# A stream of 774 unread matrix products behind the output of a two-layer transformer block

## The chip, the cores and the metric

The kernel runs on one core of one Trainium2 chip. The metric is device time in microseconds (us) of one execution. Before the change it is 1582.73 us, the median of 2 runs (1582.6 and 1582.87).

## The reference, cut to what matters

Two layers act on 512 tokens of width 1024 (`x`) and 256 context tokens (`ctx`). Layer 0 mixes tokens by a Fourier transform and a long convolution, layer 1 by latent attention; each is followed by a gated feed-forward part. Only `x` is returned.

```python
def _conv_ffn(h, w_up, conv_w, conv_b, w_down):
    gate, val = jnp.split(h @ w_up, 2, axis=-1)
    return (jax.nn.silu(_dwconv3(gate, conv_w, conv_b)) * val) @ w_down
...
        x = x + g1 * yx
        x = x + g2 * _conv_ffn(_modulate(_rms_norm(x, norm2[i]), sh2, sc2), *ffn)
...
    return x
```

The output depends on nothing that the change adds.

## The kernel before, in words

Activations lie with the 1024 channels on partitions, as eight row tiles of 128 channels each, and the tokens along the free axis. Layer 0 carries 512 tokens and 256 context tokens side by side, layer 1 from its attention on 512 tokens alone.

Nearly every product is done three times in a shortened float format (fp32r): a value is split into a high and a low part, and `mm3` (L214 to L218) issues high weight by high activation (L216), high weight by low activation (L217) and low weight by high activation (L218). Each is one weight load of 128x128 and one matmul of 512 or 256 columns. In the profile the names `wh` and `wl` are the two parts of a weight, `hh` and `hl` those of a normalised activation, `hhc` and `hlc` the same for the context, `ah` and `al` (`ahc`, `alc`) those of the feed-forward's inner activation, `Oh` and `Ol` those of the attention's output, `yh` and `yl` those of the mixer's; `mm` is a PSUM tile and `xr` a row tile of the residual.

The feed-forward part `ffn` is a loop over 22 inner tiles and two weight matrices. In layer 0 its products run in this order:

```python
                todo = [(k, q, a, n) for q in range(2) for a, n in segs for k in range(KD)]
```

`segs` is (512 columns, then 256 columns) there, so that for one weight tile 8 x 3 = 24 products of 512 columns (long ones) are followed by 24 of 256 columns (short ones), and so on, block after block.

The kernel's last work is the residual projection of layer 1 (`res_proj`, from L1167): for each of the eight row tiles products of 512 columns accumulate, then VectorE adds the result to `xr` at L1212. `build` issues one output DMA for each row tile from SyncE (L1847), then closes the pools in the reverse order of their opening. A pool is a stretch of SBUF or PSUM; closing it lets a later pool take the place, and the framework puts a semaphore wait wherever an instruction of a new tile must follow one on the old tile. On each engine instructions stand in the order in which the code issues them.

Of the kernel before, what the change touches and what calls it, by code (L numbers as in the profile page):

```python
# [9 lines left out]
F32 = mybir.dt.float32  # L10
F32R = mybir.dt.float32r
BF16 = mybir.dt.bfloat16
# [4 lines left out]
PSUM = bass.MemoryType.PSUM  # L17

P = 128
# [118 lines left out]
class Builder:  # L138
# [1703 lines left out]
    def build(self):  # L1842
        nc = self.nc
        self.setup()
        x = self.layer1(*self.layer0())
        for d in range(KD):
            nc.sync.dma_start(self.out[d], x[d][:, 0:T])  # L1847
        for n in ("xres", "h2p", "nt", "fit", "dx", "dr", "psA", "sm", "W", "P0"):
            self.close(n)

# [192 lines left out]
```

## Time and profile before

| | |
|---|---|
| median of 2 runs | 1582.73 us |
| profiled execution, its own time | 1584.1 us |
| its span, first to last instruction | 1582.3 us |
| TensorE busy | 1544.9 us, 98% of the span, 8360 matmuls |
| VectorE busy | 1028.8 us |
| ScalarE busy | 608.4 us |
| mean granted TensorE clock | 0.994 |

How to read it: "PE" is TensorE's matmul, "PEld" its weight load, DVE VectorE, ACT ScalarE, SP SyncE. A matmul's row has a start and a duration; successive matmuls overlap, since each duration contains a drain, so the pace of a stream is the distance from start to start, which I call the pitch. "PEclk" is the share of its full clock that TensorE was granted.

### The profile page before, as it was taken

The numbers are of one execution on the slowest core, as the hardware profiler recorded it, in microseconds if no ns is written. First come the engines' busy times: TensorE is split into PE (matmuls) and PEld (weight loads), VectorE is DVE, ScalarE is ACT, GpSimd is POOL, SyncE is SP. The second block draws the span as 40 slices with busy tenths as digits, with TensorE's granted clock in tenths as the row PEclk, the third lists the DMA queues.
The fourth block names the chain that finished last, engine by engine and source line by source line (L and its number), as shares of the span: only waits on it lengthen the run. The fifth ranks groups of instructions, "written<-read, shape, count | busy, mean of one in ns | idle before, by whom it ended". The sixth has DMA issues, their size and how long they took to land.

```text
span 1582.3 us, 21019 instructions
## 1 busy us (share of the span) xinstructions
PE 1544.9 (98%) x8360; PEld 1270.1 (80%) x8360; DVE 1028.8 (65%) x1740; ACT 608.4 (38%) x878; POOL 92.0 (6%) x109
## 2 busy tenths in 40 slices
PE   7999999999999999999999999999999999999999
PEld 4687888888888888888888887655459888888887
DVE  5788969878987356653364487898867544444343
ACT  4451224424332112322133247988843432233231
POOL 0013125000000000000000000111200000000000
PEclk9999999999999999999999999999999999999999
DMA  9336522543544234442353221000043232223222
GB/s 354 106 108 208 177 63 74 185 135 98 169 160 147 67 118 164 159 134 67 94 163 100 94 63 30 1 14 14 1 146 108 94 104 97 93 95 105 94 81 93
DMA packets 54542, 173.04 MB, mean 109 GB/s; under 512 B 6187, under 2 KB 9581, under 8 KB 53421
## 3 DMA queue, kind: packets, MB, share of 16 engines
q1 hardware_dynamic: 54445, 171.71, 32.8%
q8 instruction: 66, 1.08, 0.3%
q14 instruction: 31, 0.25, 0.1%
HBM read 165.91 MB, written 5.77 MB: 108 GB/s over the span
## 4 chain that ended last, share of the span: by engine, by line
PE 85%; DVE 10%; ACT 2%; DMA 2%; issue 1%; SPq 1%; POOL 0%; ACTq 0%; DVEq 0%
PE mm L216 23%; PE mm L218 23%; PE mm L217 23%; PE pv L1713 3%; PE s L1659 3%; DVE junk L301 2%; DVE wl L196 2%; PE pv L1724 1%; PE s L216 1%; PE k L216 1%; PE s L218 1%; PE s L217 1%; PE k L218 1%; PE k L217 1%; DVE hl L371 1%
## 5 line engine op out<-in xcount | busy, mean ns | idle before, releaser
L191 ACT ACTIVATE wh<-wr 128x1024 fp32r<-128x1024 f32 (+1 forms) x192 | 198.4, 1035 | 554.5 <-PE mm L217 508.4
L216 PE MATMUL mm<-hh,wh 128*128 128x512 f32 (+1 forms) x872 | 339.1, 390 | 2.5 <-ACT hh L367 0.9
L217 PE MATMUL mm<-hl,wh 128*128 128x512 f32 (+1 forms) x872 | 337.6, 387 | 2.3 <-DVE hl L371 2.3
L218 PE MATMUL mm<-hh,wl 128*128 128x512 f32 (+1 forms) x872 | 337.2, 387 | 1.6 <-DVE wl L196 1.6
L196 DVE TENSOR_TENSOR wl<-wr,wh 128x1024 fp32r<-128x1024 f32 (+2 forms) x192 | 230.5, 1203 | 140.8 <-ACT wh L191 136.6
L216 PEld LDWEIGHTS mm<-hh,wh 128*128 128x128 f32 x872 | 164.9, 189 | 35.5 <-issue 3.2
L218 PEld LDWEIGHTS mm<-hh,wl 128*128 128x128 f32 x872 | 165.0, 189 | 35.1 <-DVE wl L196 2.2
L217 PEld LDWEIGHTS mm<-hl,wh 128*128 128x128 f32 x872 | 165.1, 189 | 32.7 <-DVE hl L371 3.5
L301 DVE SCALAR_TENSOR_TENSOR junk<-wr,sb 128x1024 bf16<-128x1024 f32 x128 | 156.0, 1219 | 53.8 <-DMA wr<-wmodT 53.6
L1212 DVE SCALAR_TENSOR_TENSOR xr<-mm,mod,xr 128x512 f32<-128x512 f32 (+1 forms) x100 | 61.7, 630 | 170.1 <-PE mm L218 170.0
L217 PE MATMUL mm<-hlc,wh 128*128 128x256 f32 (+1 forms) x488 | 137.4, 282 | 0.0
L216 PE MATMUL mm<-hhc,wh 128*128 128x256 f32 (+1 forms) x488 | 137.3, 281 | 0.0
L218 PE MATMUL mm<-hhc,wl 128*128 128x256 f32 (+1 forms) x488 | 137.2, 281 | 0.0
L216 PE MATMUL mm<-ah,wh 128*128 128x512 f32 x328 | 127.6, 389 | 0.0
L217 PE MATMUL mm<-al,wh 128*128 128x512 f32 x328 | 127.6, 389 | 0.0
L218 PE MATMUL mm<-ah,wl 128*128 128x512 f32 x328 | 127.6, 389 | 0.0
L217 PEld LDWEIGHTS mm<-hlc,wh 128*128 128x128 f32 x488 | 91.6, 188 | 4.0
L216 PEld LDWEIGHTS mm<-hhc,wh 128*128 128x128 f32 x488 | 91.6, 188 | 3.9
L218 PEld LDWEIGHTS mm<-hhc,wl 128*128 128x128 f32 x488 | 93.2, 191 | 0.0
L1255 DVE TENSOR_TENSOR fg<-fg,mm 128x768 f32<-128x768 f32 (+1 forms) x44 | 36.1, 820 | 74.0 <-PE mm L218 72.3
L1253 ACT ACTIVATE fg<-fg 128x768 f32<-128x768 f32 (+1 forms) x44 | 32.5, 739 | 126.3 <-DVE fg L436 94.8
L218 PEld LDWEIGHTS mm<-ah,wl 128*128 128x128 f32 x328 | 61.6, 188 | 12.7
(395 smaller groups left out, 2721.8 us busy)
## 6 DMA issues: line engine op xcount, KB each, us to landing
wr<-w_up SPq DMA_DIRECT2D x88, 512.0 KB, 3.3
wr<-wmodT SPq DMA_DIRECT2D x80, 512.0 KB, 3.4
wr<-w_dn SPq DMA_DIRECT2D x32, 512.0 KB, 3.3
wm<-wmod0a SPq DMA_DIRECT2D x8, 1024.0 KB, 9.5
wr<-w_in SPq DMA_DIRECT2D x16, 512.0 KB, 4.3
wr<-w_out SPq DMA_DIRECT2D x13, 512.0 KB, 4.0
wr<-w_dn SPq DMA_DIRECT2D x17, 384.0 KB, 3.1
wr<-w_o SPq DMA_DIRECT2D x11, 512.0 KB, 3.9
```

Source lines behind the costliest of these rows:

```text
L191: self.nc.scalar.activation(dst, src, AF.Copy)
L196: (eng or self.nc.vector).tensor_tensor(dst, src, hi.bitcast(F32), op=ALU.subtract)
L216: mmul(out, wh, xh, start=start, stop=False)
L217: mmul(out, wh, xl, start=False, stop=False)
L218: mmul(out, wl, xh, start=False, stop=stop)
L301: nc.vector.scalar_tensor_tensor(junk, raw, 1.0, self.sb[:, j, :], op0=ALU.mult, op1=ALU.mult, accum_out=acc)
L371: return nc.vector.scalar_tensor_tensor(hl[d][:, c0 : c0 + n], box.pop(d)[:, :n], B[:, d : d + 1], hh[d][:, c0 : c0 + n].bitcast(F32), op0 ...
L1212: nc.vector.scalar_tensor_tensor(x[m][:, a2:b2], ps[:, a2 + o : b2 + o], mod[:, 8 * sec + m, c : c + 1], x[m][:, a2:b2], op0=ALU.mult, op1 ...
L1253: nc.scalar.activation(g[:, :n], g[:, :n], AF.Silu)
L1255: v.tensor_tensor(a[:, :n], g[:, :n], pss[1][:, :n], op=ALU.mult)
L1659: nc.tensor.matmul(ps, k_[0], q[0], start=True, stop=True)
L1713: nc.tensor.matmul(c.P[64 * a : 64 * a + 64, :], V[:, j, o : o + 64], c.S[a, j // 3][:, j % 3, :], start=j == 0, stop=j == 5, tile_positio ...
```

## The change

After the output DMAs have been issued, `build` closes the pools down to `psA`, calls a new function `bench`, and closes the rest behind it. `bench` opens one pool in SBUF and one in PSUM and allocates four constant tiles, filled by VectorE: `bw` (128x2048, fp32r, the weights), `bm` (128x8192, fp32r, the moving operand), and `bwb` and `bmb` (bf16), which no product reads. It then issues 774 products on constants. Nothing reads their results, which all go to two PSUM banks, and each starts and stops its own accumulation.

Row `k` of the long function X is three products of 512 columns, row `k` of the short functions Y and Z three of 256 columns, in the pattern of `mm3` (Z has the other weight first). Two rows of X come first (6 products). Then come 16 blocks of 8 long rows and 8 short rows (24 and 24 products), in eight pairs of alike blocks. The pairs differ in the offset, in columns, at which one row tile or all of them start: 48, 32 or 0 for the last, the last two or the first of the long rows, 40, 32 or 48 for the first short row, the order of weights in Z, and 16 against 112 for the short rows. In all there are 6 + 16 x 24 = 390 long and 16 x 24 = 384 short products.

```diff
-        for n in ("xres", "h2p", "nt", "fit", "dx", "dr", "psA", "sm", "W", "P0"):
+        for n in ("xres", "h2p", "nt", "fit", "dx", "dr", "psA"):
             self.close(n)
+        self.bench()
+        for n in ("mbp", "mb", "sm", "W", "P0"):
+            self.close(n)
+
+    def bench(self):
+        nc = self.nc
+        mb = self.pool("mb")
+        ps = self.pool("mbp", space=PSUM)
+        w = self.t(mb, [P, 2048], F32R, "bw")
+        m = self.t(mb, [P, 8192], F32R, "bm")
+        wb = self.t(mb, [P, 512], BF16, "bwb")
+        mbf = self.t(mb, [P, 2048], BF16, "bmb")
+        nc.vector.memset(w.bitcast(F32), 0.5)
+        nc.vector.memset(m.bitcast(F32), 0.25)
+        nc.vector.memset(wb, 0.5)
+        nc.vector.memset(mbf, 0.25)
+        o = self.t(ps, [P, 4096], F32, "bo")
+        W = lambda i, off=0, c=128, k=P: w[:k, off + 128 * i : off + 128 * i + c]
...
+        def row(k, base, lo, pitch, n, oc, d):
+            for wt, b in ((W(k), 0), (W(k), lo), (W(8 + k), 0)):
+                a = base + b + pitch * (k % 4) + d
+                nc.tensor.matmul(o[:, oc : oc + n], wt, m[:, a : a + n], start=True, stop=True)
+
+        X = lambda k, d=0: row(k, 0, 2048, 512, 512, 0, d)
+        Y = lambda k, d: row(k, 4096, 2048, 256, 256, 512, d)
+        def Z(k, d):
+            for wt, b in ((W(8 + k), 0), (W(k), 0), (W(k), 2048)):
+                a = 4096 + b + 256 * (k % 4) + d
+                nc.tensor.matmul(o[:, 512:768], wt, m[:, a : a + 256], start=True, stop=True)
+
+        for _ in range(2):
+            X(0)
+        for dx, dy in (([0] * 7 + [48], [48] * 8), ([0] * 7 + [32], [48] * 8), ([0] * 6 + [48] * 2, [48] * 8), ([0] * 8, [40] + [48] * 7),
+                       ([0] * 8, [32] + [48] * 7), ([48] + [0] * 7, [48] * 8)):
+            for _ in range(2):
+                for k in range(8):
+                    X(k, dx[k])
+                for k in range(8):
+                    Y(k, dy[k])
+        for _ in range(2):
+            for k in range(8):
+                X(k)
+            for k in range(8):
+                Z(k, 48)
+        for _ in range(2):
+            for k in range(8):
+                X(k)
+            for k in range(8):
+                Y(k, 16 if k < 1 else 112)
```

TensorE's instructions at the end of the program before, where `mm` is the PSUM tile of the last residual row tile:

```order
L217 MATMUL mm_13295<-al_13032,wh_13291 128x512
L218 MATMUL mm_13295<-ah_13031,wl_13292 128x512
L216 MATMUL mm_13295<-ah_13103,wh_13291 128x512
L217 MATMUL mm_13295<-al_13104,wh_13291 128x512
L218 MATMUL mm_13295<-ah_13103,wl_13292 128x512
L2039 UNCONDITIONAL_BRANCH
```

The program ends with that last product on TensorE. At the same place after the change, where `bo` is the PSUM tile of the new products:

```order
L216 MATMUL mm_13295<-ah_13103,wh_13291 128x512
L217 MATMUL mm_13295<-al_13104,wh_13291 128x512
L218 MATMUL mm_13295<-ah_13103,wl_13292 128x512
L1879 MATMUL bo_13346<-bm_13339,bw_13338 128x512 [waits DVE_49]
L1879 MATMUL bo_13346<-bm_13339,bw_13338 128x512 x29
L1879 MATMUL bo_13346<-bm_13339,bw_13338 128x256 x24
L1879 MATMUL bo_13346<-bm_13339,bw_13338 128x512 x24
```

The new stream stands behind everything that TensorE had, and its first product alone has a wait, for VectorE.

VectorE's end before, with the last two additions to the residual:

```order
L196 TENSOR_TENSOR wl_13292<-wr_13289,wh_13291 128x768 [waits DMAHW4_49,Activation_49]
L1212 TENSOR_SCALAR xr_1767_10380<-mm_13243,mod_5_74,xr_1767_10380 128x512 [waits PE_49]
L1212 TENSOR_SCALAR xr_1768_10381<-mm_13269,mod_5_74,xr_1768_10381 128x512 [waits PE_49]
L1212 TENSOR_SCALAR xr_1769_10382<-mm_13295,mod_5_74,xr_1769_10382 128x512 [waits PE_49]
L2039 UNCONDITIONAL_BRANCH
```

VectorE has nothing behind the last addition here. After the change:

```order
L1212 TENSOR_SCALAR xr_1768_10381<-mm_13269,mod_5_74,xr_1768_10381 128x512 [waits PE_49]
L1212 TENSOR_SCALAR xr_1769_10382<-mm_13295,mod_5_74,xr_1769_10382 128x512 [waits PE_49]
L1862 MEMSET bw_13338 128x2048
L1863 MEMSET bm_13339 128x8192
L1864 MEMSET bwb_13340 128x512
L1865 MEMSET bmb_13341 128x2048 [waits DMAHW3_49,DMAHW1_49]
L2096 UNCONDITIONAL_BRANCH
```

The four fills stand behind the last residual addition. The first two, which the products read, wait for nothing but their turn; the last one waits for output DMAs. SyncE's output DMAs and all instructions of ScalarE and GpSimd stand as before.

More of the change, by code (lines that the diff above doesn't have):

```diff
@@ L1847, in build, with run @@
             nc.sync.dma_start(self.out[d], x[d][:, 0:T])
-        for n in ("xres", "h2p", "nt", "fit", "dx", "dr", "psA", "sm", "W", "P0"):
+        for n in ("xres", "h2p", "nt", "fit", "dx", "dr", "psA"):
             self.close(n)
+        self.bench()
[15 more added lines that the diff above has]
+        W = lambda i, off=0, c=128, k=P: w[:k, off + 128 * i : off + 128 * i + c]
+        M = lambda off, n=512, k=P: m[:k, off : off + n]
+        O = lambda b=0, n=512, c=P: o[:c, 512 * b : 512 * b + n]
+        def run(f, n=10, start=False):
+            for i in range(n):
+                a, b, c = f(i)
+                nc.tensor.matmul(a, b, c, start=i == 0 or start, stop=i == n - 1 or start)
+        def row(k, base, lo, pitch, n, oc, d):
[27 more added lines that the diff above has]
+                Y(k, 16 if k < 1 else 112)
```

## The prediction

> **What bounds the kernel now.** I read the page's busy times and slices first, then the end of the timeline, since that is where the new work is put.
>
> ```profile
> span 1582.3 us, 21019 instructions
> PE 1544.9 (98%) x8360; PEld 1270.1 (80%) x8360; DVE 1028.8 (65%) x1740; ACT 608.4 (38%) x878; POOL 92.0 (6%) x109
> PE   7999999999999999999999999999999999999999
> ...
> PE 85%; DVE 10%; ACT 2%; DMA 2%; issue 1%; SPq 1%; POOL 0%; ACTq 0%; DVEq 0%
> ```
>
> TensorE is busy for 98% of the span and makes up 85% of the chain of waits. There is no room beside it, and the program's order gives none either: the new products stand behind all of TensorE's work. So whatever they take is added at the end. The timeline there:
>
> ```profile
> 1578.08 0.39 PE L218 MATMUL mm<-ah,wl 128*128 128x512 f32 x1
> 1578.51 0.75 DVE L1212 SCALAR_TENSOR_TENSOR xr<-mm,mod,xr 128x512 f32<-128x512 f32 x1 [3.33 <-PE mm L218]
> 1579.28 0.33 SPq L1847 DMA_DIRECT2D out_dram<-xr  x1
> ...
> out_dram<-xr SPq DMA_DIRECT2D x8, 256.0 KB, 2.0
> ```
>
> TensorE ends at 1578.08 + 0.39 = 1578.47, VectorE at 1578.51 + 0.75 = 1579.26, the last output DMA is issued at 1579.28 and lands 2.0 later (the median of the eight), at 1581.28. The program's closing waits take the rest to 1582.3, some 1.0 us.
>
> **The fills.** The products read `bw` and `bm`, which VectorE fills behind its last addition: 2048 + 8192 = 10240 columns. The trace has small fills only:
>
> ```profile
> 0.80 0.09 DVE L252 MEMSET ones<- 128x32 f32 x1 [0.80 <-PEq L2036]
> 0.89 0.27 DVE L258 MEMSET sT<- 128x256 f32 x1
> 1.11 0.07 DVE L509 MEMSET on<- 128x1 f32 x2
> 1.18 0.27 DVE L522 MEMSET s<- 128x256 f32 x1
> ```
>
> By their durations 224 columns more (256 against 32) cost 0.27 - 0.09 = 0.18 us, 0.8 ns each, and the two fills would take 8.2 us. But these rows overlap: `sT` ends at 0.89 + 0.27 = 1.16 when the next fill has begun at 1.11. By the ends, `sT` takes from the end of `ones` (0.89) to 1.16, 0.27 us, and `s` from the end of `on` (1.18) to 1.45, 0.27 us again. Two fills in a row that take 0.27 us each from end to end give 1.05 ns a column, and 10240 x 1.05 = 10.7 us. I take the ends, because work that starts before its forerunner is done can't be charged by its duration, and keep 8.2 as the lower bound; for the upper one 11.5, by adding 8% for rows rounded to 10 ns. The Trainium skill (VectorE: DVE Perf Modes, "Zero memsets can be issued as uint32 (trn2)") has a fill at one cycle per element whatever the type, and the page's table a clock of 0.96 GHz; by that estimate the two fills take 10.7 us, and the durations' 8.2 would make the sum 2.5 us shorter. The ends in this trace agree with the page, the durations don't.
>
> The fills of `bwb` and `bmb` run beside the products; the last waits for output DMAs that land by 1581.28, long before VectorE gets to it. Nothing waits behind it. They cost nothing as long as the products last longer than some 3 us.
>
> From VectorE's end to TensorE's start I take a pair of rows where a product waits for a weight's low part:
>
> ```profile
> 1180.94 1.23 DVE L196 TENSOR_TENSOR wl<-wr,wh 128x1024 fp32r<-128x1024 f32 x1 [3.25 <-ACT wh L191]
> 1182.22 0.38 PE L218 MATMUL mm<-Oh,wl 128*128 128x256 f32 x1 [0.76 <-DVE wl L196]
> ```
>
> 1180.94 + 1.23 = 1182.17, so 0.05 us. The first product then starts at 1579.26 + 10.7 + 0.05 = 1590.0.
>
> **The products.** Layer 0's feed-forward part is the same stream: blocks of 24 long and 24 short products in the order high, high, low, without a wait. Sixteen such blocks stand between 389.66 and 521.93, as many as the change has:
>
> ```profile
> 389.66 0.39 PE L216 MATMUL mm<-hh,wh 128*128 128x512 f32 x1
> ...
> 395.10 0.28 PE L216 MATMUL mm<-hhc,wh 128*128 128x256 f32 x1
> 395.22 0.28 PE L217 MATMUL mm<-hlc,wh 128*128 128x256 f32 x1
> ...
> 521.93 0.39 PE L216 MATMUL mm<-ah,wh 128*128 128x512 f32 x1
> ```
>
> ```profile
> 389.66:521.93 132.27, 132.27 (x771) 117.30 (x769) 107.55 (x203) 40.45 (x51) 0.00 (x0) 1.00 0.46 152
> ```
>
> The second fence is the row of that stretch in the table by stages (length, then TensorE's busy time and count; the 1.00 is the granted clock). 24 long products take 395.10 - 389.66 = 5.44 us, a pitch of 226.7 ns; a block takes 132.27 / 16 = 8.267, so its short part 2.83 us, a pitch of 117.8 ns. The 16 blocks then cost 132.27 us and the six long products ahead of them 6 x 0.2267 = 1.36, together 133.6 us. The last product's row is 0.28 long, 0.16 more than its pitch.
>
> Two other paces bound this. Short products also run faster: from 1190.28 to 1190.96, over 6 products, the pitch is 113 ns in a stretch of attention output. And long ones also run slower: 178 products in 41.28 us, 231.9 ns, in the mixer's output.
>
> ```profile
> 1190.28 0.28 PE L216 MATMUL mm<-Oh,wh 128*128 128x256 f32 x1
> ...
> 1190.96 0.28 PE L216 MATMUL mm<-Oh,wh 128*128 128x256 f32 x1
> ...
> 302.15:343.43 41.28, 41.28 (x178) 33.49 (x179) 29.85 (x54) 9.51 (x12) 0.00 (x0) 1.00 0.65 215
> ```
>
> The blocks differ from each other only in the seam, and what a seam can do is to bring one pace or the other. At most this is 384 x (117.8 - 113.3) = 1.7 us less and 390 x (231.9 - 226.7) = 2.0 us more. I take zero for it: the trace's sixteen seams of this kind all stay at 8.267.
>
> **The clock.** Behind the last old product TensorE stands idle from 1578.47 to 1590.0, 11.5 us. The trace has four stretches at half clock inside the kernel (granted clock third from the end), and the first row here is what stood ahead of the longest:
>
> ```profile
> 1211.13:1214.55 3.42, 1.79 (x16) 1.59 (x15) 3.42 (x6) 1.89 (x4) 0.00 (x0) 1.00 0.14 23
> ...
> 26.71:30.13 3.42, 3.42 (x14) 1.77 (x17) 0.61 (x2) 1.06 (x1) 0.00 (x0) 0.50 1.05 432
> 245.17:251.99 6.82, 6.82 (x31) 6.53 (x30) 6.03 (x12) 3.25 (x7) 6.64 (x4) 0.50 0.26 80
> 961.97:965.38 3.41, 3.19 (x10) 3.19 (x11) 0.95 (x1) 1.66 (x3) 0.00 (x0) 0.50 0.00 0
> 1214.55:1221.38 6.83, 6.83 (x34) 6.83 (x34) 3.51 (x15) 0.00 (x0) 0.00 (x0) 0.50 0.65 219
> ...
> 1215.59 0.41 PE L217 MATMUL mm<-hl,wh 128*128 128x256 f32 x1
> ...
> 1221.14 0.40 PE L218 MATMUL mm<-hh,wl 128*128 128x256 f32 x1
> ```
>
> TensorE was busy for 1.79 of 3.42 us there, and half clock followed; after 11.5 us without any product I expect it all the more. The four last 3.4 or 6.8 us. In the last one 26 short products take 1221.14 - 1215.59 = 5.55 us, 213 ns each; a long one at half clock would then take some 427 ns, an estimate by twice the columns, and a microsecond at half clock loses 1 - 227/427 = 0.47 us. So the new stream opens at half clock; I take 5.1 us of it, the middle of the two lengths, and 2.4 us of loss. Bounds: 2 us (0.9 lost), as the end of such a stretch need not wait for our start, and 10 us (4.7 lost).
>
> **The sum.** Start 1590.0, products 133.6, half clock 2.4, last row 0.16: the last product ends at 1726.2. For the close I take 0.8 us, since the waits for DMAs are long met, with 0.3 and 1.1 (the 1.0 above) as bounds. Span 1727.0, that is 144.7 over 1582.3. The profiled execution's own time was 1584.1, but the median stands at 1582.73, 0.4 over the span; on that median the time is 1727.4 us.
>
> **The rivals.**
>
> *The seams bring the fast pace.* Every block's short part runs at 113 ns: -1.7, 1725.7 us. For it speaks that the fast stretch exists with the same shape; against it that none of sixteen seams in the trace led there. 0.13.
>
> *The long products take the slow pace* of the mixer's output: +2.0, 1729.4 us. For it: it lasted 178 products there. Against: the feed-forward's do not. 0.07.
>
> *The fills go by their rows' durations*: 8.2 instead of 10.7, 1724.9 us. 0.12.
>
> *The clock alone sets the pace.* These products add nothing up; if the rest beyond the columns fell away, a product at full clock would take half of what the half clock shows, 107 and 213 ns: 390 x 0.2133 + 384 x 0.1067 = 124.2, 9.4 less, 1718.0 us. The first matmul of an accumulation runs in the trace like the others (395.10 to 395.22 is 0.12 us), which speaks against it. 0.03. The Trainium skill (TensorE: Matmul & The Clock Gate, "Back-to-back issue gap") states N/2.4 + 2.5 ns, 215.8 and 109.2 ns, by which I estimate 126.1 us of products and a time of 1719.9; the trace's 226.7 and 117.8 disagree with it.
>
> *Not slower: the unread work doesn't run.* If something between program and chip dropped what nobody reads, only VectorE's fills would be left, 12800 columns x 1.05 = 13.4 us behind 1579.26, a span of 1593.5 and a time of 1593.9, 0.7% over. It decides as long as fewer than some 120 of the 774 run: 2% is 31.7 us, of which idle, half clock and close take 1590.0 + 2.4 + 0.16 + 0.8 - 1582.3 = 11.1, and (31.7 - 11.1) / (133.6 / 774) = 119. Against it stands a small instruction whose result is never read either, an exponential issued to load its table, and which ran:
>
> ```profile
> L1693 ACT ACTIVATE padq<-ones x1: 202/202/202, 963.5 to 963.5; 128x1 f32<-128x1 f32 x1
> ```
>
> 0.01.
>
> **How the numbers follow.** The forecast, 1727.4, has 0.64; its own terms reach from -1.5 and -0.5 (clock, close) to +2.3, +0.8 and +0.3 (clock, fills, close), which won't all meet. The range from 1724.4 to 1730.4 takes in the fast seams, the slow long pace and the fills by their durations, and leaves out the clock-only pace, the dropped work and a half clock at its longest, together under 2 in 10. A measurement of this kernel tells some 2% from no change. All cases but the dropped work are more than 8% slower: slower 0.99, within 2% 0.01, faster 0.
>
> **What would show it.** In the profile after: fills of `bw` and `bm` that end near 1589.9, TensorE idle for 11.5 us and its first new product near 1590.0; half clock in the first 2 to 10 us of the stream and 1.00 from there; blocks of 8.27 us, long at 226.7 and short at 117.8 ns, alike within each pair; the last product's end near 1726.2 and the span's end within 1 us behind it. A block of 8.16 would be the fast seam, one of 8.39 the slow long pace. I am wrong if the stream starts some 2.5 us earlier (the fills), if blocks stand at 7.68 us (the clock alone), or if waits stand between products.

## The result and the profile after

The changed kernel takes 1725.68 us, the median of 2 runs (1725.06 and 1726.31), against 1582.73 before: a ratio of 1.0907, interval 1.0884 to 1.0930. (The quotient of two medians can differ by up to 0.0005 from a ratio given with an interval; here it is 1.0903.) The medians differ by 142.95 us; 144.7 were forecast, and a time of 1727.4.

The page of the profile after: its span, the busy times, and the slices of TensorE and of the granted clock.

```profile
span 1724.5 us, 22573 instructions
PE 1678.5 (97%) x9134; PEld 1388.4 (81%) x9134; DVE 1039.2 (60%) x1744; ACT 608.2 (35%) x878; POOL 92.0 (5%) x109
PE   7999998999999999999999999999999999997999
...
PEclk9999999999999999999999999999999999998999
```

There are 9134 - 8360 = 774 matmuls more: nothing was dropped. The one new dip that the clock shows as well as TensorE's row is the fourth slice from the end, where the old work ends and the new stream begins. (The 8 in TensorE's seventh slice has none in the clock's row; the slices are longer than before, so they do not cover the same work.) The timeline of VectorE there, then TensorE's last old and first new product:

```profile
1576.00 0.75 DVE L1212 SCALAR_TENSOR_TENSOR xr<-mm,mod,xr 128x512 f32<-128x512 f32 x1 [3.33 <-PE mm L218]
1577.13 1.76 DVE L1862 MEMSET bw<- 128x2048 f32 x1 [0.38 <-issue]
1580.55 6.88 DVE L1863 MEMSET bm<- 128x8192 f32 x1 [1.65 <-issue]
```

```profile
1575.58 0.39 PE L218 MATMUL mm<-ah,wl 128*128 128x512 f32 x1
1587.49 0.79 PE L1879 MATMUL bo<-bm,bw 128*128 128x512 f32 x1 [11.53 <-DVE bm L1863]
```

Read the fills by their ends: `bw` ends at 1577.13 + 1.76 = 1578.89, 2.14 us behind the last addition (1576.75), and `bm` at 1587.43, another 8.54 us: 1.04 ns a column in both. The gaps ahead of the rows (0.38 and 1.65, put down to "issue") are what the durations leave out. The product starts 10.74 us behind the addition; 10.75 were forecast.

The stages of the new stream: the stretch at half clock, then the second block of each of the eight pairs (the columns are the length, then each engine's busy time and count, then the granted clock third from the end), and at last the whole stream.

```profile
1587.49:1592.52 5.03, 5.03 (x12) 3.97 (x13) 2.25 (x2) 0.00 (x0) 0.00 (x0) 0.50 0.00 0
1599.53:1607.74 8.21, 8.21 (x51) 7.24 (x49) 0.00 (x0) 0.00 (x0) 0.00 (x0) 1.00 0.01 2
1616.03:1624.36 8.33, 8.33 (x50) 7.33 (x49) 0.00 (x0) 0.00 (x0) 0.00 (x0) 1.00 0.01 2
1632.62:1640.84 8.22, 8.22 (x50) 7.23 (x49) 0.00 (x0) 0.00 (x0) 0.00 (x0) 1.00 0.00 0
1649.04:1657.23 8.19, 8.19 (x50) 7.24 (x49) 0.00 (x0) 0.00 (x0) 0.00 (x0) 1.00 0.00 0
1665.52:1673.81 8.29, 8.29 (x51) 7.34 (x49) 0.00 (x0) 0.00 (x0) 0.00 (x0) 1.00 0.01 2
1682.11:1690.42 8.31, 8.31 (x51) 7.33 (x49) 0.00 (x0) 0.00 (x0) 0.00 (x0) 1.00 0.01 2
1698.68:1706.95 8.27, 8.27 (x50) 7.33 (x49) 0.00 (x0) 0.00 (x0) 0.00 (x0) 1.00 0.00 0
1715.22:1723.49 8.27, 8.27 (x50) 7.29 (x48) 0.00 (x0) 0.00 (x0) 0.00 (x0) 1.00 0.00 0
...
1587.49:1723.49 136.00, 136.00 (x774) 119.66 (x774) 2.25 (x2) 0.00 (x0) 0.00 (x0) 0.98 0.00 1
```

Half clock lasts 5.03 us (5.1 forecast), the stream 136.0 (133.6 + 2.4 = 136.0 forecast). The blocks are not alike: they run from 8.19 to 8.33 us around the 8.267 of layer 0's feed-forward part, so the seams do matter, both ways. (The blocks' ends are read from the starts of the products.)

### The profile page after: what moved, and what is told of

Its sections match the earlier page's. It is cut to its first block, busy times and chain, and to the rows that moved or that the text cites. A ratio compares the mean times of both kernels' runs of the same rounds, so it can differ in the third digit from the quotient of the medians.

```text
span 1724.5 us, 22573 instructions
## 1 busy us (share of the span) xinstructions
PE 1678.5 (97%) x9134; PEld 1388.4 (81%) x9134; DVE 1039.2 (60%) x1744; ACT 608.2 (35%) x878; POOL 92.0 (5%) x109
## 4 chain that ended last, share of the span: by engine, by line
PE 85%; DVE 9%; DMA 3%; ACT 1%; issue 1%; POOL 0%; SPq 0%; DVEq 0%; ACTq 0%
PE mm L216 21%; PE mm L218 21%; PE mm L217 21%; PE bo L1879 8%; PE pv L1713 2%; PE s L1659 2%; DVE junk L301 2%; DVE wl L196 1%; PE pv L1724 1%; PE s L216 1%; PE k L216 1%; PE s L218 1%; PE s L217 1%; PE k L217 1%; PE k L218 1%
## 5 line engine op out<-in xcount | busy, mean ns | idle before, releaser
L1879 PE MATMUL bo<-bm,bw 128*128 128x512 f32 (+1 forms) x726 | 130.8, 343 | 11.5 <-DVE bm L1863 11.5
L1879 PEld LDWEIGHTS bo<-bm,bw 128*128 128x128 f32 x726 | 113.9, 190 | 28.1 <-DVE bm L1863 11.9
```

What stands on the lines that cost most here:

```text
L1879: nc.tensor.matmul(o[:, oc : oc + n], wt, m[:, a : a + n], start=True, stop=True)
```

## The experiments

My theory: the change costs the fills by their ends, half clock because TensorE stands idle meanwhile, and the stream at the feed-forward's pace. The rivals: fills by their durations; half clock that belongs to the new products rather than to the idle time; and, for the blocks' differences, a pace that hangs on the place in the stream instead of on the seam. The first two experiments take the first terms apart, the next four the seams, and the last two carry the seams into the kernel itself.

**The fills alone** (`e1_fills_only`).

```diff
-        for _ in range(2):
-            X(0)
...
-                Y(k, 16 if k < 1 else 112)
```

> Leaves out all 774 products; the four fills stay. The theory of the prediction (a fill costs what lies between the ends of its rows, 1.05 ns a column) expects the last fill to end 13.4 us behind the last residual addition and the time to rise by 11.2 us over the kernel before (13.4 + 0.8 for the close - the 3.04 us that stood behind that addition before): near 1594. The rival, that fills cost what their rows last (0.84 ns a column), expects 10.8 us and a rise of 8.6: near 1591.3. That the products were never the cost would show as a time near 1725.

1593.64 us against 1582.81 for the kernel before on the same chip, a ratio of 1.0073 (1.0054 to 1.0091): 10.8 us more. Its last addition and its fills on VectorE:

```profile
1576.66 0.75 DVE L1212 SCALAR_TENSOR_TENSOR xr<-mm,mod,xr 128x512 f32<-128x512 f32 x1 [3.33 <-PE mm L218]
1577.79 1.76 DVE L1862 MEMSET bw<- 128x2048 f32 x1 [0.38 <-issue]
1581.21 6.88 DVE L1863 MEMSET bm<- 128x8192 f32 x1 [1.66 <-issue]
1588.15 0.48 DVE L1864 MEMSET bwb<- 128x512 bf16 x1
1589.01 1.76 DVE L1865 MEMSET bmb<- 128x2048 bf16 x1 [0.38 <-issue]
```

From 1577.41 to 1589.01 + 1.76 = 1590.77 are 13.36 us; 13.4 were expected by the ends, 10.8 by the durations. The durations fall: they add up to 10.88 us in a stretch that lasts 13.36. The span ends at 1591.7, 0.9 behind the last fill.

**The fills early** (`e2_fills_early`): GpSimd fills the two tiles ahead of the last feed-forward part; the two tiles that no product reads are left out.

```diff
         self.close("pa")
+        mb = self.pool("mb", side="right")
+        self.bw = self.t(mb, [P, 2048], F32R, "bw")
+        self.bm = self.t(mb, [P, 8192], F32R, "bm")
+        nc.gpsimd.memset(self.bw.bitcast(F32), 0.5)
+        nc.gpsimd.memset(self.bm.bitcast(F32), 0.25)
...
```

> The two tiles that products read are filled by GpSimd ahead of the last feed-forward part, the two that none reads are left out, and the products are as in the changed kernel. TensorE then stands still only for the last residual addition, some 1.2 us. The theory (10.7 us of fills, and half clock because TensorE stood idle for them) expects no half clock and a stream of 133.6 us: a rise of 133.6 + 0.16 + 0.8 - 3.04 = 131.5 us over the kernel before, near 1714.3. The rival, that half clock comes with these products themselves (constant operands, a new stream) and not from the idle time, expects 2.4 us more, near 1716.7, with a stretch at 0.50 in the first microseconds of the stream. If GpSimd's fills disturb VectorE in the last feed-forward part, waits on VectorE appear there.

1715.71 us, a ratio of 1.0840 (1.0822 to 1.0858). The last addition, the first new products, and the stages of the first 3.4 us and of the whole stream:

```profile
1577.83 0.75 DVE L1212 SCALAR_TENSOR_TENSOR xr<-mm,mod,xr 128x512 f32<-128x512 f32 x1 [3.33 <-PE mm L218]
...
1578.73 1.38 PE L1876 MATMUL bo<-bm,bw 128*128 128x512 f32 x5 [0.94 <-DVE xr L1212]
...
1578.73:1582.14 3.41, 3.41 (x15) 2.85 (x16) 0.00 (x0) 0.00 (x0) 0.00 (x0) 1.00 0.20 77
...
1578.73:1712.33 133.60, 133.60 (x774) 117.91 (x774) 0.00 (x0) 0.00 (x0) 0.00 (x0) 1.00 0.01 3
```

With an idle stretch of 0.94 us in place of 11.5 the same products start at full clock, and the stream lasts 133.60 us: 2.4 less than in the changed kernel, and what was expected to the tenth. The half clock belongs to the idle time, and it comes ahead of the new products: over the idle 10.74 us of the changed kernel the granted clock is 0.60 on the mean, and in `e1_fills_only`, which has no product to offer, it is 0.58 on the mean from 1577.41 to 1591.70.

The median of whole runs is 132.9 over before, between the two expectations, 131.5 and 134, so the trace has to decide. It also shows a cost of this version ahead of the new products. While GpSimd fills `bm`, an instruction of VectorE on 128x2 numbers, 0.17 us long in the changed kernel, stands for 3.48 us:

```profile
1212.39 6.93 POOL L1842 MEMSET bm<- 128x8192 f32 x1
...
1215.87 3.48 DVE L225 TENSOR_SCALAR rq_i<-nrm_s 128x2 int32<-128x2 int32 x1
```

It ends at 1219.35, 0.03 us behind the fill. TensorE's old products run 0.5 us behind those of the changed kernel at 1185 us and 1.8 us behind them from 1224 us to the end, with a stretch at half clock of 3.4 us between in both; so this costs some 1.3 us, about what parts 132.9 from 131.5. That the fill holds VectorE up is read from these two rows of one execution, and whole runs of one kernel spread over several us (before: 1579.43 to 1584.48), so the agreement is no proof.

**One seam for all blocks** (`e3_all_last48`, `e4_all_last32`): every block gets the seam of the first pair, or of the second.

```diff
-        for dx, dy in (([0] * 7 + [48], [48] * 8), ([0] * 7 + [32], [48] * 8), ([0] * 6 + [48] * 2, [48] * 8), ([0] * 8, [40] + [48] * 7),
-                       ([0] * 8, [32] + [48] * 7), ([48] + [0] * 7, [48] * 8)):
+        for dx, dy in (([0] * 7 + [48], [48] * 8),) * 8:
...
```

> All 16 blocks have the seam of the first pair (the last long row 48 columns on). The theory that the seam sets the pace of the short products expects all 16 short parts at 113.8 ns (2.73 us) and blocks of 8.21 us, as in the first pair of the changed kernel. The rival, that the pace hangs on the place in the stream (early blocks fast, late ones slow), expects the first blocks at 2.73 and the later ones at 2.83.

> All 16 blocks have the seam of the second pair (the last long row 32 columns on). The theory that the seam sets the pace expects all 16 short parts at 117.7 ns (2.83 us) and blocks of 8.33 us, so that this stream is 16 x 0.12 = 1.9 us longer than that of the run with 48. The rival, the place in the stream, expects the first two blocks at 2.73.

One run each, 1728.34 and 1730.84 us. These totals say nothing of the seams: the new stream starts 3.6 and 4.3 us later than in the changed kernel (1591.11 and 1591.81 against 1587.49), since the old part took longer. An early block, the last block and the stream of the run with 48, then those of the run with 32:

```profile
1602.41:1610.62 8.21, 8.21 (x51) 7.24 (x49) 0.00 (x0) 0.00 (x0) 0.00 (x0) 1.00 0.01 2
1717.31:1725.51 8.20, 8.20 (x50) 7.20 (x48) 0.00 (x0) 0.00 (x0) 0.00 (x0) 1.00 0.00 0
1591.11:1725.51 134.40, 134.40 (x774) 118.16 (x774) 2.25 (x2) 0.00 (x0) 0.00 (x0) 0.99 0.00 1
```

```profile
1603.08:1611.41 8.33, 8.33 (x50) 7.33 (x49) 0.00 (x0) 0.00 (x0) 0.00 (x0) 1.00 0.01 2
1719.66:1727.98 8.32, 8.32 (x50) 7.29 (x48) 0.00 (x0) 0.00 (x0) 0.00 (x0) 1.00 0.00 0
1591.81:1727.98 136.17, 136.17 (x774) 119.56 (x774) 2.25 (x2) 0.00 (x0) 0.00 (x0) 0.99 0.00 1
1591.81:1594.97 3.16, 3.16 (x8) 2.48 (x9) 2.25 (x2) 0.00 (x0) 0.00 (x0) 0.50 0.00 0
```

First and last block are alike in each run, 8.2 and 8.3. The streams differ by 1.8 us, where 1.9 were expected. The rival, the place in the stream, falls. The last row is the run's half clock: 3.16 us here, against 5.03 in the changed kernel, after the same fills.

**A map of the seam** (`e5_map_last`, `e6_map_short`).

```diff
+        for dx, dy in [([0] * 7 + [d], [48] * 8) for d in (0, 16, 32, 48, 64, 80, 96, 112)]:
...
```
```diff
+        for dx, dy in [([0] * 8, [f] + [d] * 7) for f, d in ((0, 0), (16, 16), (32, 32), (48, 48), (64, 64), (44, 48), (8, 0), (24, 16))]:
...
```

> Eight pairs of blocks, alike but for the start of the last long row: 0, 16, 32, 48, 64, 80, 96, 112 columns on (the short rows all at 48). Known from the run before: 48 gives short parts of 2.73 us, 32 of 2.83. The theory that only the place within 64 columns (256 bytes) counts expects 112 as 48 (2.73), 96 as 32 (2.83), 64 as 0 and 80 as 16. If the jump between two rows alone counted, in columns of any size, 64 to 112 would be unlike the first four. Offset 0 is the seam of layer 0's feed-forward part and should give 2.83 and long parts of 5.44.

> Eight pairs of blocks with all long rows at 0: all short rows at 0, 16, 32, 48 or 64 columns, then the first short row at 44 with the others at 48, at 8 with 0, and at 24 with 16. The theory that the seam sets the pace by its place within 64 columns expects the pair with 64 as that with 0, and 48 as in the feed-forward part (2.83 us). The last three have a first row that does not start at a multiple of 16 columns, like 40 before 48 in the changed kernel, which gave 2.74: if it is such a row that throws the stream into the fast pace, all three stand at 2.74; if it is the distance of 8 columns to the next row, the pairs with 8 and 24 do not.

The second block of each pair in the first map (last long row at 0, 16, 32, 48, 64, 80, 96, 112):

```profile
1600.57:1608.83 8.26, 8.26 (x50) 7.33 (x49) 0.00 (x0) 0.00 (x0) 0.00 (x0) 1.00 0.01 2
1617.12:1625.41 8.29, 8.29 (x51) 7.33 (x49) 0.00 (x0) 0.00 (x0) 0.00 (x0) 1.00 0.01 2
1633.69:1642.02 8.33, 8.33 (x51) 7.34 (x49) 0.00 (x0) 0.00 (x0) 0.00 (x0) 1.00 0.00 0
1650.25:1658.46 8.21, 8.21 (x51) 7.24 (x49) 0.00 (x0) 0.00 (x0) 0.00 (x0) 1.00 0.00 0
1666.74:1675.01 8.27, 8.27 (x51) 7.33 (x49) 0.00 (x0) 0.00 (x0) 0.00 (x0) 1.00 0.01 2
1683.29:1691.58 8.29, 8.29 (x50) 7.33 (x49) 0.00 (x0) 0.00 (x0) 0.00 (x0) 1.00 0.01 2
1699.86:1708.19 8.33, 8.33 (x51) 7.33 (x49) 0.00 (x0) 0.00 (x0) 0.00 (x0) 1.00 0.00 0
1716.43:1724.63 8.20, 8.20 (x50) 7.20 (x48) 0.00 (x0) 0.00 (x0) 0.00 (x0) 1.00 0.00 0
```

The lower four repeat the upper four: 8.26, 8.29, 8.33, 8.21 and 8.27, 8.29, 8.33, 8.20. So of these eight places only the one within 64 columns, 256 bytes, counts. The same for the second map (all short rows at 0, 16, 32, 48, 64; then the first at 44 before 48, at 8 before 0, at 24 before 16):

```profile
1600.06:1608.40 8.34, 8.34 (x51) 7.38 (x49) 0.00 (x0) 0.00 (x0) 0.00 (x0) 1.00 0.01 2
1616.69:1625.00 8.31, 8.31 (x50) 7.34 (x49) 0.00 (x0) 0.00 (x0) 0.00 (x0) 1.00 0.01 2
1633.36:1641.71 8.35, 8.35 (x50) 7.37 (x49) 0.00 (x0) 0.00 (x0) 0.00 (x0) 1.00 0.00 0
1650.03:1658.29 8.26, 8.26 (x50) 7.33 (x49) 0.00 (x0) 0.00 (x0) 0.00 (x0) 1.00 0.00 0
1666.61:1674.94 8.33, 8.33 (x50) 7.37 (x49) 0.00 (x0) 0.00 (x0) 0.00 (x0) 1.00 0.01 2
1683.23:1691.49 8.26, 8.26 (x50) 7.33 (x49) 0.00 (x0) 0.00 (x0) 0.00 (x0) 1.00 0.00 0
1699.80:1708.14 8.34, 8.34 (x50) 7.38 (x49) 0.00 (x0) 0.00 (x0) 0.00 (x0) 1.00 0.00 0
1716.47:1724.79 8.32, 8.32 (x50) 7.31 (x48) 0.00 (x0) 0.00 (x0) 0.00 (x0) 1.00 0.00 0
```

The pair at 64 repeats the pair at 0 (8.33 and 8.34). 48 is the best of the plain places, and the feed-forward part uses it: a gap of 192 bytes (`hgap` in the code) stands ahead of its short row tiles. No unaligned first row of these three brings the fast pace (8.26, 8.34, 8.32), so the 8.19 of 40 before 48 isn't the work of just any row that doesn't start at a multiple of 16 columns. A distance of 8 columns doesn't bring it by itself either: it is there in the last two pairs. But there the first row lies 8 columns on, and not 8 back as with 40 before 48, and the other rows lie at 0 and 16. Which property of 40 does it stays open.

**The seams in the kernel** (`e7_kernel_last48`, `e8_kernel_first40`): the kernel before, with no new products and some row tiles of layer 0's feed-forward part moved in SBUF (all others keep their place within 256 bytes). In the first, `hh7` and `hl7` lie 192 bytes on:

```diff
...
+                if d == KD - 1:
+                    self.t(hx, [P, 48], F32, f"{n}pa")
                 ts.append(Two(self.t(hx, [P, T], F32R, f"{n}{d}"), self.t(hc, [P, C], F32R, f"{n}c{d}")))
+            self.t(hx, [P, 16], F32, f"{n}pb")
```

In the second, `hhc0` and `hlc0` lie 32 bytes back:

```diff
-        self.gap("hgap", 192)
+        self.gap("hgap", 160)
...
+            if n == "hl":
+                self.t(hc, [P, 56], F32, "hlpa")
             for d in range(KD):
                 ts.append(Two(self.t(hx, [P, T], F32R, f"{n}{d}"), self.t(hc, [P, C], F32R, f"{n}c{d}")))
+                if d == 0:
+                    self.t(hc, [P, 8], F32, f"{n}pb")
```

> The kernel before, without any new products; the last long row tiles (hh7 and hl7) of layer 0's feed-forward part lie 192 bytes on, which makes each seam from 512 to 256 columns in its 42 plain up-projection blocks that of the first pair of the changed kernel. The theory that a seam sets the pace by its place in SBUF expects these blocks at 8.21 us instead of 8.27 (short parts 2.73 instead of 2.83, long parts 5.475 instead of 5.44), 42 x 0.06 = 2.5 us less in all, a ratio of 0.9984. The rival, that in a working kernel other engines' reads or waits set the pace, or that accumulation does, expects blocks at 8.27 and a ratio of 1.

> The kernel before, without any new products; the first short row tiles (hhc0 and hlc0) lie 32 bytes back, the seam of the fourth pair of the changed kernel (40 before 48). The theory expects the 42 blocks at 8.19 us instead of 8.27 (short parts 2.74, long parts 5.455), 42 x 0.073 = 3.1 us less, a ratio of 0.998. [...]

Eleven runs of each and 21 of the kernel before: 1580.30 us against 1582.62, a ratio of 0.9985 (0.9975 to 0.9995), and 1579.88, a ratio of 0.9978 (0.9968 to 0.9988). 0.9984 and 0.998 were expected. Both gains are far below 2%, but their intervals leave out 1. One block of the first, and then its sixteen blocks that took 132.27 us before:

```profile
386.98:395.19 8.21, 8.21 (x50) 7.24 (x49) 7.08 (x11) 3.84 (x5) 0.00 (x0) 1.00 0.39 130
...
386.98:518.28 131.30, 131.30 (x770) 115.79 (x769) 107.58 (x203) 40.46 (x51) 0.00 (x0) 1.00 0.47 153
```

And of the second:

```profile
399.44:407.63 8.19, 8.19 (x50) 7.24 (x49) 8.19 (x17) 3.08 (x5) 0.00 (x0) 1.00 0.39 128
...
391.22:522.35 131.13, 131.13 (x771) 115.91 (x770) 107.50 (x203) 40.23 (x51) 0.00 (x0) 1.00 0.47 153
```

The blocks stand at 8.21 and 8.19 with VectorE and ScalarE busy beside them and with products that accumulate, so neither sets the pace. All 42 plain blocks stand there within 0.03 us in both traces, not only these sixteen; at 0.06 and 0.073 us each that makes 2.5 and 3.1 us, and the medians fell by 2.3 and 2.7. The second version is the fastest here: 0.22% under the kernel before by the ratio, 0.17% by the medians.

## Why the prediction was right

It was right in its sum and in all its steps but one: the zero for the seams came from two effects that cancel, and not from the reason given. Counted from the last residual addition, whose row ends at 1576.75, to the end of the span at 1724.5, the changed kernel has 147.75 us; the kernel before had 3.04 there. The difference, 144.7 us, is the 144.7 of the sum. That they agree to the tenth is luck, as the half clock and the seams show.

- *The fills*, 10.7 us: the addition's end to the first product is 10.74 with the handover. `e1_fills_only` confirms the ends and refutes the durations. The two unread fills cost nothing, since the stream outlasts them.
- *The products*, 133.6 us: 133.60 in `e2_fills_early`, where no half clock is in the way (the seams are in it).
- *The half clock*, 2.4 us: 136.0 - 133.6 = 2.4 in the changed kernel, and its cause, the idle time, is shown by `e2_fills_early` and by the clock of `e1_fills_only`. The size was a middle value and could have been another: the five streams with the same fills show 3.2 us of it (`e4_all_last32`) to 5.8; the longest is this stretch of `e6_map_short`:

```profile
1587.53:1593.34 5.81, 5.81 (x14) 4.55 (x15) 2.25 (x2) 0.00 (x0) 0.00 (x0) 0.50 0.00 0
```

The traces show what the length hangs on. Inside each trace the granted clock changes only on a grid of 3.4133 us: the starts and ends of the four stretches at half clock before (30.13, 245.17, 251.99, 961.97, 965.38, 1214.55, 1221.38) lie 1, 64, 66, 274, 275, 348 and 350 such steps behind 26.71. In the changed kernel the stream starts 1.62 us ahead of a step (1589.11) and is granted full clock at the step after that, 1.62 + 3.41 = 5.03 us on. In `e4_all_last32` it starts 0.25 us behind a step (1591.56) and has full clock from the next, 3.16 us on. The grid lies elsewhere in each execution (the step near 962 is at 961.97 before, 961.06 after and 963.08 in `e3_all_last48`), so the length is a matter of chance, and a middle value is what a forecast can take.

- *The close*, 0.8 us: 1724.5 less the last product's end (1723.49 + 0.16 = 1723.65) is 0.85.
- *The seams*, zero: the sum was right and the reason was not. I took zero because the trace's sixteen seams all stay at 8.267 us. The change's seams do not. Three of the eight pairs have the fast short pace that I held for a rival; this is the short part of the first block of the first pair, 24 products in 2.73 us, 113.8 ns each, where 2.83 were forecast:

```profile
1596.80:1599.53 2.73, 2.73 (x25) 2.73 (x24) 0.00 (x0) 0.00 (x0) 0.00 (x0) 1.00 0.00 0
```

And six pairs have long products mostly at 228 to 239 ns, about the pace of the other rival, in one to four rows beside the seam. The eight blocks quoted above add up to 66.09 us, and eight of the old kind would be 66.14. The gain of the one and the loss of the other cancel, which no row of before could have told.

The median, 1725.68, is also what the rival of the fast seams gave, 1725.7. The blocks decide against it: five of the eight pairs keep the slow short pace. Nor did the clock alone set the pace, by which a block would take 7.68 us; none takes less than 8.19.

What remains of the 1.7 us between 1727.4 and 1725.68 lies ahead of the change: the last old product starts at 1575.58 in the profile after and at 1578.08 before, 2.5 us earlier, of which 0.8 comes back because the median stands 1.2 over the profiled span after and 0.4 over it before. The old part starts its first product 1.07 us earlier, and its stretch at half clock near 1214 lasts 3.4 us instead of 6.83:

```profile
1213.64:1217.06 3.42, 3.42 (x18) 3.42 (x18) 3.07 (x14) 0.00 (x0) 0.00 (x0) 0.50 0.80 286
```

That is the spread of this kernel from run to run, which a sum on one profiled execution cannot see.

## What to carry to other kernels

Work appended behind the end of this kernel could be priced to within 2 us of 145, because the trace held the same stream elsewhere, the fills were counted from end to end, and the idle time ahead of the stream was charged with a stretch at half clock. The rest is chance: where the clock's grid lies, and how the old part runs. Where blocks of products of two widths alternate, as here, the place of the row tiles at the seam, within 256 bytes, can set the pace of the whole part behind it; measure a few places on constants, and then move the real tiles.

## What the runs showed of the hardware that was not expected

A stream of 24 short products (128x256) with the same arguments took 113.8 or 117.8 ns each on the mean, and which of the two hung on the place of a single row tile ahead of it. After the first few products the pace stays, and it is the same in all 16 blocks of `e3_all_last48` (2.73 us) and in all 16 of `e4_all_last32` (2.83). In the maps, places 256 bytes apart gave the same. With all short rows at 0 in `e6_map_short` there is a third pace, 119.7 ns. Why TensorE keeps the pace that it falls into is not shown by these runs.

The rows of VectorE's fills last 0.84 ns a column (6.88 us for 8192), while their ends lie 1.04 ns a column apart. Half clock did not follow an idle stretch of 0.94 us; after one of some 11.5 us it lasted 3.2 to 5.8 us into the new stream, always to a step of the clock's grid of 3.4133 us.
